# Attention mixer of an encoder trunk: where the two halves of a unit's output are added, and when the output is split

## The chip, the cores and the metric

The kernel runs on one core of a Trainium2 chip. The metric is device microseconds of one execution, as the median of several runs; profiled executions are recorded by the hardware profiler, one at a time.

## What is computed

Two layers of an encoder trunk run on two sequences (512 and 256 tokens, width 1024) with shared weights. Each layer is `x += ½FFN; x += Mixer; x += ½FFN`, each behind an RMSNorm. Layer 0 mixes with a gated linear recurrence, layer 1 with windowed attention; the change lies in the latter:

```python
def window_gqa_mixer(x, w_qkv, w_o, sinks):        # 16 query heads, 4 key heads, d = 64
    q, k, v = split(x @ w_qkv); q, k = rope_partial(q), rope_partial(k)
    # blocks of 128 queries against the block before, their own and the one after
    s = einsum('bnqhgd,bnkhd->bnhgqk', qb, kband) * d**-0.5
    s = where(|kpos - qpos| <= 128, s, -inf)
    m = maximum(max(s), sink); p = exp(s - m)
    o = einsum('bnhgqk,bnkhd->bnqhgd', p / (sum(p) + exp(sink - m)), vband)
    return o.reshape(B, T, 1024) @ w_o
```

All arithmetic is float32 by demand of accuracy. TensorE works on float32r, a shortened form, so every operand is split into a high part `hi` (a cast on ScalarE) and a rest `lo = x - hi` (a subtraction on VectorE), and a product takes two or three matmuls.

## The kernel before

The attention stage (`swa`) starts with the projections of keys and values. Then one hand-made pipeline (`pipeline`) runs 24 units, in each of which one group of four query heads that share a key head meets one block of 128 queries: for each of 4 groups `g`, four blocks of the long sequence and two of the short one. A unit's parts are set on steps, unit `i` starting at step `4 i`:

- `query`, `turn`: split and transpose the queries (`qT`, a buffer of tag `tA`).
- `scores` (L1380, L1381): score matmuls into PSUM, and from there by VectorE (L1383) into a score buffer of tag `big`, with mask and maximum.
- `exps` (L1396) on ScalarE, `sink`, `denominator`: the normalisation runs on GpSimd (L1412), four instructions a unit.
- `probs`, steps 7 to 9: the probabilities are transposed on TensorE (L1418) and split (`split`, L319 and L320) into two `tA` buffers for each block of keys.
- `values`: two matmuls per block of keys (L1430, L1431) accumulate in one PSUM bank, `po`. Its partitions 0 to 63 hold the result with the high part of the values, 64 to 127 that with the low part.
- `finish`, at step `4 i + 8` plus the number of key blocks (2 or 3): ScalarE copies the lower half to partitions 0 to 63 of a `tA` buffer `low` (L1436), and VectorE adds the two halves in two instructions (L1441), even heads to partitions 0 to 63 and odd heads to 64 to 127 of the group's output tile `of`, a `big` buffer.

Between these parts stand the `extra` pieces with steps of their own: the query projection in pieces of six matmuls (the second half of it from step 18 on, every second step, to step 66), a reload of x from DRAM, the output splits and, from step 66 on, 24 pieces of the output projection `out_proj` for its first half, which reads groups 0 and 1. `split_out` casts a group's `of` into high and low parts of two new `big` tiles (L1254 on ScalarE, L1255 on VectorE, four of each for one group). The groups are split at steps 60, 65 and 84, and group 3 behind the pipeline, ahead of the second half of `out_proj`.

The list of events, sorted by step, gives the program order. The framework takes that order as priority, and lays out the queue of each engine by it, by what its own model of durations says is ready, and by which buffers are free: the `big` tag has 21 (h, the normalised input of the projections, takes 8 until the last query block is done), `tA` has 8, PSUM 8 banks. Each engine then works its queue in order. DMAs started on SP or ScalarE are plain; `into` (L147) starts one on GpSimd that adds to its destination. SP's queue also carries all weight loads (L160), and ScalarE and VectorE split the loaded weights (L175, L176).

Of the kernel before, what the change touches and what calls it, by code (L numbers as in the profile page):

```python
# [9 lines left out]
F32 = mybir.dt.float32  # L10
F32R = mybir.dt.float32r
# [5 lines left out]
P = 128  # L17
# [5 lines left out]
T = TA + TB  # L23
# [6 lines left out]
HD = 64  # L30
# [3 lines left out]
SEQS = ((0, TA), (TA, TB))  # L34
# [18 lines left out]
class Trunk:  # L53
# [1129 lines left out]
    def swa(self, next_row):  # L1183
        nc = self.nc
        self.load_bands()
        self.later(self.spill_x)
        kT = [self.big([P, 2, T], F32R) for _ in range(KV)]
        vv = [self.big([P, 3, KV, P], F32R) for _ in range(2)]

        def put_kv(s, b, ps):  # L1190
            off, n = SEQS[s]
            gb = off // P + b
            st = self.big([P, KV, 2, P], F32R)
            kh, kl = st[:, :, 0, :], st[:, :, 1, :]
            k = self.tmp(256)
            self.rotate(ps[:, :256], KV, b, k)
            self.split(k.rearrange("p (h d) -> p h d", d=HD), kh[:, :, :HD], kl[:, :, :HD])
            nc.scalar.copy(kh[:, :, HD:], kh[:, :, :HD].bitcast(F32))
            nc.scalar.copy(kl[:, :, HD:], kl[:, :, :HD].bitcast(F32))
            src = ps[:, 256:].rearrange("p (g d) -> p g d", d=HD)  # L1200
            v = vv[gb // 3][:, gb % 3]
            nc.scalar.copy(v[:, :, :HD], src)
            nc.vector.tensor_sub(v[:, :, HD:], src, v[:, :, :HD].bitcast(F32))

            def rest():
                for g in range(KV):
                    pt = self.ps(256)
                    for i in range(2):
                        self.transpose_r(pt[:, i * P : (i + 1) * P], st[:, g, i, :])
                    nc.scalar.copy(kT[g][:, :, gb * P : (gb + 1) * P], pt.rearrange("p (a b) -> p a b", a=2))  # L1210

            return rest

        self.drain(self.proj_tok("kv", put_kv))
        qtok = {}

        def put_q(half):
            def f(s, b, ps):
                gb = SEQS[s][0] // P + b
                if half and gb % 3 == 0:  # L1220
                    hold.append(self.big([P, 3, 512]))
                t = hold[gb // 3][:, gb % 3] if half else self.xt()[:, :512]
                self.rotate(ps, 512 // HD, b, t)
                for gg in range(2):
                    qtok[(s, b, half * 2 + gg)] = t[:, gg * 256 : (gg + 1) * 256]

            hold = []
            return f

        tiles = [None] * NC  # L1230
        of = {}

        def units(gs):
            def alloc(g):
                if g not in of:
                    of[g] = self.big([P, 2, T])
                return of[g]

            for g in gs:
                for s, (off, n) in enumerate(SEQS):  # L1240
                    for b in range(n // P):
                        q = lambda s=s, b=b, g=g: qtok[(s, b, g)]
                        yield Unit(self, s, b, g, q, kT, vv, lambda g=g: alloc(g))

        def split_out(gs):
            for g in gs:
                for i in range(2):
                    for s, (off, n) in enumerate(SEQS):
                        if s == 0:
                            tiles[2 * g + i] = self.big([P, 2, T], F32R)  # L1250
                        t = tiles[2 * g + i]
                        hi, lo = t[:, 0, off : off + n], t[:, 1, off : off + n]
                        src = of[g][:, i, off : off + n]
                        nc.scalar.copy(hi, src)  # L1254
                        nc.vector.tensor_sub(lo, src, hi.bitcast(F32))  # L1255

        q = itertools.chain(self.proj_tok("q0", put_q(0)), self.proj_tok("q1", put_q(1)))
        wo = self.out_proj("sw_o", 0, tiles, None)
        for _ in range(8):
            next(q)  # L1260
        piece = lambda g: lambda: next(g, None)
        extra = [(i * 5 / 4 - 4, piece(q)) for i in range(16)]
        extra += [(18 + 2 * i, piece(q)) for i in range(25)]
        extra.append((46, self.reload_x))
        extra.append((60, lambda: split_out((0,))))
        extra.append((65, lambda: split_out((1,))))
        extra += [(66 + i * 3 / 2, piece(wo)) for i in range(24)]
        extra.append((84, lambda: split_out((2,))))
        self.pipeline(list(units(range(KV))), extra)
        split_out((3,))  # L1270
        self.drain(wo)
        self.drain(self.out_proj("sw_o", 1, tiles, next_row))

# [44 lines left out]
    def pipeline(self, units, extra):  # L1318
        events = []

        def at(step, rank, *calls):
            events.append((step, rank, len(events), calls))

        for i, u in enumerate(units):
            t = 4 * i
            at(t - (3 if i else 5), 5, u.query)
            at(t - 2, 3.5, u.turn)
            for h in range(GQ):
                at(t + h // 2, 0, lambda u=u, h=h: u.scores(h))
            at(t + 2, 2, u.sink)  # L1330
            for h in range(GQ):
                at(t + 1 + h // 2, 2, lambda u=u, h=h: u.exps(h))
            at(t + 2, 2, u.denominator)
            for j in range(u.nkb):
                at(t + 7 + j, 1, lambda u=u, j=j: u.probs(j))
                at(t + 9 + j, 4, lambda u=u, j=j: u.values(j))
            at(t + 8 + u.nkb, 4, u.finish)
        for step, call in extra:
            at(step, 3, call)
        for _, _, _, calls in sorted(events, key=lambda e: e[:3]):  # L1340
            for c in calls:
                c()


class Unit:
# [87 lines left out]
    def finish(self):  # L1433
        k, nc = self.k, self.k.nc
        low = k.tmp(512)
        nc.scalar.copy(low[:HD, :], self.po[HD:, :])  # L1436
        of = self.of()
        lo = self.off + self.b * P
        for par in range(2):
            r = lambda t: t.rearrange("p (c a q) -> p c a q", a=2, q=P)[:, :, par, :]  # L1440
            nc.vector.tensor_add(of[par * HD : (par + 1) * HD, :, lo : lo + P], r(self.po[:HD, :]), r(low[:HD, :]))  # L1441
# [114 lines left out]
```

## Time and profile before

| | |
|---|---|
| time, median of 3 runs | 2774.59 us (2774.25 to 2774.86) |
| the profiled execution | 2774.57 us, of it 2772.5 us span |
| granted TensorE clock | 0.999 |
| PE busy | 2747.2 us, 99% of the span |
| DVE / ACT / POOL busy | 2220.5 / 1389.7 / 410.5 us |
| attention units, first to last score matmul | 2063.8 to 2228.6 us |
| L1441, the additions of `finish` | 48 of 414 ns |

PE is TensorE's matmuls, PEld its weight loads, DVE VectorE, ACT ScalarE, POOL GpSimd, SP the SyncE that starts most DMAs. In the stretches of time, each engine's busy us are followed by the number of its instructions. In the rows of groups the busy total and the mean of one come first, behind the second bar the engine's idle time just before them and what ended it. In the timeline, the first figure is the start and the second the duration, both in us, and in square brackets stands how long the engine had been idle.

### The profile page before, as it was taken

What the parts mean: (1) busy time and instruction counts of PE and PEld (TensorE: products, weight loads), DVE (VectorE), ACT (ScalarE), POOL (GpSimd) and SP (SyncE); (2) the same over time, 40 slices, a digit from 0 to 9 for tenths busy, and PEclk for the clock granted to TensorE, in tenths of its full rate; (3) what the DMA queues carried; (4) which work ended last, traced back from release to release, by engine and by line L of the source; (5) the groups of instructions that cost most, each with busy time, mean ns of one, the idle gap of its engine ahead of it and who ended that gap; (6) DMA issues with size and microseconds to landing.
All of it is one profiled execution on the core that took longest, in us unless ns stands there. A gap on an engine that the chain in (4) does not pass through costs nothing.

```text
span 2772.5 us, 40790 instructions
## 1 busy us (share of the span) xinstructions
PE 2747.2 (99%) x15117; PEld 2554.7 (92%) x15117; DVE 2220.5 (80%) x3808; ACT 1389.7 (50%) x2589; POOL 410.5 (15%) x449
## 2 busy tenths in 40 slices
PE   8999999999999999999999999999999999999998
PEld 8999999989999889999999999999888789999998
DVE  8788788767887788788878888887848878788877
ACT  7344444734455674444445544444558865444443
POOL 2111121200000101221111121111102211211111
PEclk9999999999999999999999999999999999999999
DMA  6554554851123743555444365544412122655443
GB/s 172 130 126 114 128 138 122 232 155 39 39 62 71 206 116 80 137 137 133 115 115 124 75 147 133 128 116 115 133 66 77 47 65 73 145 133 129 120 112 107
DMA packets 339943, 319.71 MB, mean 115 GB/s; under 512 B 12872, under 2 KB 259104, under 8 KB 339744
## 3 DMA queue, kind: packets, MB, share of 16 engines
q1 hardware_dynamic: 296992, 221.81, 27.2%
q0 software_dynamic: 38448, 81.81, 16.2%
q10 hardware_dynamic: 4304, 13.49, 1.3%
q8 instruction: 119, 1.95, 0.3%
q14 instruction: 80, 0.66, 0.1%
HBM read 225.82 MB, written 15.73 MB: 87 GB/s over the span
## 4 chain that ended last, share of the span: by engine, by line
PE 95%; DVE 2%; ACT 1%; DMA 0%; issue 0%; DVEq 0%; ACTq 0%; SPq 0%
PE ps L513 42%; PE ps L577 21%; PE ps L315 6%; PE ps L314 6%; PE ps L316 6%; PE ps L760 5%; PE ps L823 3%; PE ps L928 1%; PE ps L1418 1%; PE ps L904 1%; PE ps L385 1%; PE ps L1430 0%; PE ps L1380 0%; PE ps L1381 0%; PE ps L1431 0%; PE ps L1181 0%
## 5 line engine op out<-in xcount | busy, mean ns | idle before, releaser
L513 PE MATMUL ps<-big,w 128*128 128x384 f32 x6720 | 1169.3, 334 | 0.0
L513 PEld LDWEIGHTS ps<-big,w 128*128 128x128 f32 x6720 | 1165.9, 188 | 1.7 <-ACT tA L530 0.2
L208 ACT CAST w<-wr 128x512 fp32r<-128x512 f32 x600 | 415.7, 707 | 687.2 <-PE ps L513 279.8
L577 PE MATMUL ps<-w,big 128*128 128x512 f32 x2520 | 575.3, 389 | 0.0
L577 PEld LDWEIGHTS ps<-w,big 128*128 128x128 f32 x2520 | 472.7, 188 | 97.5
L209 DVE TENSOR_TENSOR w<-wr,w 128x512 fp32r<-128x512 f32 (+1 forms) x520 | 437.8, 846 | 147.5 <-ACT w L208 131.5
L599 DVE SCALAR_TENSOR_TENSOR x<-ps,x 128x512 f32<-128x512 f32 x468 | 302.0, 684 | 10.0 <-PE ps L316 9.9
L147 POOL DMA_DIRECT2D s<-wr x126 | 110.5, 884 | 1243.1 <-DMA s<-in_ffn_w_dram 432.8
L314 PE MATMUL ps<-big,w 128*128 128x384 f32 x640 | 219.6, 345 | 1.2 <-ACT w L175 0.9
L315 PE MATMUL ps<-big,w 128*128 128x384 f32 x640 | 215.7, 337 | 0.8 <-DVE big L320 0.8
L316 PE MATMUL ps<-big,w 128*128 128x384 f32 x640 | 214.4, 335 | 0.0
L319 ACT CAST big<-tA 128x384 fp32r<-128x384 f32 x296 | 148.0, 513 | 113.4 <-DVE tA L552 36.2
L760 PE MATMUL ps<-w,big 128*128 128x512 f32 x756 | 177.2, 392 | 0.1
L320 DVE TENSOR_TENSOR big<-tA,big 128x384 fp32r<-128x384 f32 x296 | 169.2, 582 | 6.6 <-ACT big L319 4.6
L147 POOL DMA_DIRECT2D wr<-wr x109 | 95.8, 879 | 524.1 <-DMA wr<-in_ffn_w_dram 191.2
L760 PEld LDWEIGHTS ps<-w,big 128*128 128x128 f32 x756 | 140.5, 188 | 29.2 <-DVE w L320 0.6
L209 POOL TENSOR_TENSOR w<-wr,w 128x512 fp32r<-128x512 f32 x80 | 138.5, 1732 | 195.2 <-ACT w L208 192.2
L215 DVE TENSOR_TENSOR wr<-wr,wr 128x512 f32<-128x512 f32 (+1 forms) x120 | 121.1, 1009 | 24.9 <-issue 21.1
L314 PE MATMUL ps<-w,big 128*128 128x512 f32 x336 | 134.6, 401 | 0.3 <-DVE big L1441 0.2
L316 PE MATMUL ps<-w,big 128*128 128x512 f32 x336 | 132.2, 393 | 0.6 <-DVE big L400 0.5
L315 PE MATMUL ps<-w,big 128*128 128x512 f32 x336 | 131.7, 392 | 0.0
L315 PEld LDWEIGHTS ps<-big,w 128*128 128x128 f32 x640 | 120.5, 188 | 2.1 <-DVE big L320 2.0
(215 smaller groups left out, 3465.8 us busy)
## 6 DMA issues: line engine op xcount, KB each, us to landing
wr<-in_ffn_w_dram SPq DMA_DIRECT2D x264, 512.0 KB, 4.0
s<-wr POOLq DMA_DIRECT2D x126, 256.0 KB, 4.9
s<-in_ffn_w_dram SPq DMA_DIRECT2D x120, 256.0 KB, 3.3
wr<-wr POOLq DMA_DIRECT2D x80, 256.0 KB, 3.8
wr<-in_hg_w_in_dram SPq DMA_DIRECT2D x32, 512.0 KB, 3.9
wr<-wr POOLq DMA_DIRECT2D x29, 512.0 KB, 4.6
spill<-x ACTq DMA_DIRECT2D x12, 512.0 KB, 4.0
kept<-big POOLq DMA_DIRECT2D x8, 768.0 KB, 9.7
```

What stands on the lines that cost most here:

```text
L147: self.nc.gpsimd.dma_start(out, src, accum_op=ALU.add)
L208: nc.scalar.copy(h, src)
L209: (eng or nc.vector).tensor_sub(l, src, h.bitcast(F32))
L314: nc.tensor.matmul(out, a[0], b[0], start=first, stop=False)
L315: nc.tensor.matmul(out, a[0], b[1], start=False, stop=False)
L316: nc.tensor.matmul(out, a[1], b[0], start=False, stop=last)
L319: self.nc.scalar.copy(hi, src)
L320: self.nc.vector.tensor_sub(lo, src, hi.bitcast(F32))
L513: self.nc.tensor.matmul(ps, a[x], b[y], start=first and k == 0 and i == 0, stop=k == 3 and i == 2, skip_group_check=True,)
L577: nc.tensor.matmul(ps, a[x], w[y], start=name == chain and kp == 0 and q == 0, stop=kp == 1 and q == 2, skip_group_check=True,)
L599: self.nc.vector.scalar_tensor_tensor(x, ps, c, x, ALU.mult, ALU.add)
L760: nc.tensor.matmul(ps, x[:, sl], y, start=fresh and k == 0 and q == 0, stop=k == 3 and q == 2, skip_group_check=True,)
```

## The change

For the first 21 units, `finish` copies all 128 partitions of `po` to `low` with one ScalarE instruction. Then, for even and odd heads, a plain DMA on SP writes the upper half of `low` to its place in `of`, and an accumulating DMA on GpSimd adds the lower half to it; each moves 64 partitions of 256 elements. The last three units keep the copy and the two VectorE additions.

`split_out` now does one tile and one sequence at a time. The twelve pieces of groups 0 to 2 stand at steps 50, 52, 54, 56; 58, 60, 62, 64; and 83, 85, 87, 89. Group 3's four pieces stay behind the pipeline.

```diff
-        def split_out(gs):
-            for g in gs:
-                for i in range(2):
-                    for s, (off, n) in enumerate(SEQS):
-                        if s == 0:
-                            tiles[2 * g + i] = self.big([P, 2, T], F32R)
-                        t = tiles[2 * g + i]
-                        hi, lo = t[:, 0, off : off + n], t[:, 1, off : off + n]
-                        src = of[g][:, i, off : off + n]
-                        nc.scalar.copy(hi, src)
-                        nc.vector.tensor_sub(lo, src, hi.bitcast(F32))
+        def split_out(g, i, s):
+            off, n = SEQS[s]
+            if s == 0:
+                tiles[2 * g + i] = self.big([P, 2, T], F32R)
+            hi, lo = (tiles[2 * g + i][:, half, off : off + n] for half in range(2))
+            self.split(of[g][:, i, off : off + n], hi, lo)
...
-        extra.append((60, lambda: split_out((0,))))
-        extra.append((65, lambda: split_out((1,))))
+        for n in range(12):
+            extra.append(((50, 58, 83)[n // 4] + 2 * (n % 4), lambda n=n: split_out(n // 4, n // 2 % 2, n % 2)))
         extra += [(66 + i * 3 / 2, piece(wo)) for i in range(24)]
-        extra.append((84, lambda: split_out((2,))))
         self.pipeline(list(units(range(KV))), extra)
-        split_out((3,))
+        for n in range(4):
+            split_out(3, n // 2, n % 2)
...
         for i, u in enumerate(units):
             t = 4 * i
+            u.moved = i < 21
...
     def finish(self):
         k, nc = self.k, self.k.nc
         low = k.tmp(512)
-        nc.scalar.copy(low[:HD, :], self.po[HD:, :])
         of = self.of()
         lo = self.off + self.b * P
+        if self.moved:
+            nc.scalar.copy(low, self.po)
+            for par in range(2):
+                r = lambda t: t.rearrange("p (c a q) -> p c a q", a=2, q=P)[:, :, par, :]
+                dst = of[par * HD : (par + 1) * HD, :, lo : lo + P]
+                nc.sync.dma_start(dst, r(low[:HD, :]))
+                k.into(dst, r(low[HD:, :]))
+            return
+        nc.scalar.copy(low[:HD, :], self.po[HD:, :])
         for par in range(2):
             r = lambda t: t.rearrange("p (c a q) -> p c a q", a=2, q=P)[:, :, par, :]
             nc.vector.tensor_add(of[par * HD : (par + 1) * HD, :, lo : lo + P], r(self.po[:HD, :]), r(low[:HD, :]))
```

## The prediction

> **What bounds the kernel now.** I read the page's head and chain first, to see which engine has to be relieved for anything to count.
>
> ```profile
> span 2772.5 us, 40790 instructions
> PE 95%; DVE 2%; ACT 1%; DMA 0%; issue 0%; DVEq 0%; ACTq 0%; SPq 0%
> ```
>
> The chain is TensorE's from end to end: 95% of the span. The change takes no matmul away, so all it can give back is time in which TensorE stands still inside the attention stage, and all it can cost is new time of that kind. So next comes the stage itself, cut into stretches of 20 us.
>
> ```profile
> core 0: us, PE busy (x) PEld busy (x) DVE busy (x) ACT busy (x) POOL busy (x), PEclk, DMA share, GB/s
> 2080.00:2100.00 20.00, 19.04 (x112) 15.85 (x110) 17.31 (x50) 16.59 (x42) 5.59 (x9) 1.00 0.33 106
> 2100.00:2120.00 20.00, 19.37 (x116) 16.50 (x114) 14.92 (x53) 16.41 (x47) 6.09 (x14) 1.00 0.24 80
> 2140.00:2160.00 20.00, 19.89 (x117) 17.08 (x116) 16.55 (x59) 16.40 (x48) 6.59 (x14) 1.00 0.01 2
> 2160.00:2180.00 20.00, 17.08 (x94) 13.22 (x92) 18.65 (x55) 18.87 (x49) 4.10 (x8) 1.00 0.31 105
> 2180.00:2200.00 20.00, 19.37 (x109) 15.94 (x110) 17.44 (x55) 14.68 (x43) 5.52 (x12) 1.00 0.00 1
> 2200.00:2220.00 20.00, 20.00 (x115) 17.05 (x114) 17.46 (x49) 16.29 (x43) 5.58 (x8) 1.00 0.23 67
> ```
>
> The other stretches of the stage have PE at 20.00. PE misses 0.96 + 0.63 + 0.11 + 2.92 + 0.63 = 5.25 us, over half of it in 2160 to 2180, where DVE and ACT are both above 18.6 of 20. The waits and the timeline say what happens there.
>
> ```profile
> PE ps L1431 <- DVE tA L320: 2.2, 2, 1.9
> PE ps L1380 <- ACT tA L1371: 0.7, 2, 0.5
> 2170.04 0.39 PE L316 MATMUL ps<-w,big 128*128 128x512 f32 x1
> 2172.32 0.50 PE L1431 MATMUL ps<-tA,big 128*128 128x512 f32 x1 [1.89 <-DVE tA L320]
> 2167.76 1.22 DVE L176 TENSOR_TENSOR w<-wr,w 128x1024 fp32r<-128x1024 f32 x1
> 2168.89 1.96 DVE L1255 TENSOR_TENSOR big<-big,big 128x512 fp32r<-128x512 f32 x4
> 2171.58 0.69 DVE L320 TENSOR_TENSOR tA<-ps,tA 128x512 fp32r<-128x512 f32 x1
> 2179.95 1.95 DVE L1255 TENSOR_TENSOR big<-big,big 128x512 fp32r<-128x512 f32 x4
> ```
>
> The value matmul L1431 waits 1.89 us for the low half of a probability tile (L320). DVE made that late because it had a weight split (L176, 1.22 us) and the four output-split subtractions of group 0 in one lump (L1255, 1.96 us) in front of it. The second lump, group 1's, stands at 2179.95.
>
> Busy time hides a little more: matmuls of this shape start 0.23 us apart in the next fence, so after 2170.04 the next was due at 2170.27 and 2.05 us were lost, 0.16 more than the idle shown. The waits of PE in the stage are nine, so the ceiling of any gain is about 5.25 + 9 x 0.16 = 6.7 us, 0.24% of the run.
>
> ```profile
> 2148.18 0.39 PE L315 MATMUL ps<-w,big 128*128 128x512 f32 x1
> 2148.41 0.40 PE L316 MATMUL ps<-w,big 128*128 128x512 f32 x1
> ```
>
> The Trainium skill, "Perfetto Trace Analysis", section "Identifying the Most-Contended Engine", says that matmul busy time is a bad measure and that weight-load busy time is the better one. By that rule, with the full stretch's PEld of 17.05 as 100%, the four short stretches up to 2200 would lose about 1.4, 0.6, 4.5 and 1.3 us, 7.8 in all, and the ceiling would be 1.1 us higher; no run here shows which is nearer.
>
> The profiled execution took 2774.57 us, 2.07 more than its span; it lies at the median of the three runs (2774.59), so sums made on the trace are put on 2774.6. A difference of 0.2%, 5.5 us, is about what a measurement of this kernel can tell from no change.
>
> **The change part by part.** First the finish of a unit, 21 times.
>
> ```profile
> L319 ACT CAST tA<-ps 128x512 fp32r<-128x512 f32 x56 | 32.7, 585 | 8.7 <-PE ps L1418 8.1
> L1436 ACT COPY tA<-ps 64x512 f32<-64x512 f32 x24 | 14.0, 583 | 3.3 <-PE ps L1431 2.8
> L1441 DVE TENSOR_TENSOR big<-ps,tA 64x256 f32<-64x256 f32 x48 | 19.9, 414 | 4.7 <-ACT tA L1436 4.3
> ```
>
> The ACT copy grows from 64 to 128 partitions. A 128x512 eviction takes 585 ns where the 64x512 one takes 583, so this costs nothing. DVE loses 2 x 414 ns per unit, 42 x 0.414 = 17.4 us over some 140 us; none of it is TensorE time except where DVE is late. The po bank in PSUM comes free after the copy and no longer after the two additions.
>
> In their place stand 42 plain transfers on SP and 42 accumulating ones on GpSimd, 64 KB each. The nearest rows:
>
> ```profile
> big<-in_rope_dram ACTq DMA_DIRECT2D x1, 64.0 KB, 1.9
> wr<-in_sw_w_o_dram SPq DMA_DIRECT2D x8, 512.0 KB, 3.7
> L147 POOL DMA_DIRECT2D s<-wr x126: 855/872/1202, 25.9 to 2712.6; - x126
> DMA to landing us min/median/max: 3.2/4.6/10.7
> 2163.66 11.67 SPq L160 DMA_DIRECT2D wr<-in_sw_w_o_dram  x4
> 2151.79 1.84 POOL L1412 TENSOR_SCALAR big<-big,stat 128x256 f32<-128x256 f32 x4 [3.78 <-DVE stat L1409]
> 2156.48 2.27 POOL L1412 TENSOR_SCALAR big<-big,stat 128x384 f32<-128x384 f32 x4 [2.85 <-PE ps L1418]
> ```
>
> A plain transfer lands in 1.9 us (64 KB) to 3.7 us (512 KB); I take 2, by the row of the same size. An accumulating one occupies GpSimd for 0.87 us and lands 3.2 to 10.7 us later; I take 4, between the smallest and the median, since those rows carry four times the bytes. From the copy's start to the landed sum: 0.58 + 2 + 2 x 0.87 + 4 = 8.3 us, against 0.58 + 0.83 = 1.4 now.
>
> Who is behind these waits? On SP, a plain transfer waits for the copy, and the weight loads stand behind it; there are four of them in 11.67 us, so they have room. On GpSimd, an accumulating transfer waits for the plain one, and behind it stand the next unit's normalisations (L1412). GpSimd is idle 2.85 to 3.78 us between their groups in these rows and needs 1.74 of it. The next copy starts beside a group (2156.37 and 2156.48 below), so the plain transfer lands about when that group ends: hidden, bounds 0 and 2 us per unit, of which I take 0 for most and 0.4 us over the whole stage.
>
> ```profile
> 2156.37 0.58 ACT L1436 COPY tA<-ps 64x512 f32<-64x512 f32 x1
> 2164.18 0.58 ACT L1436 COPY tA<-ps 64x512 f32<-64x512 f32 x1
> ```
>
> Who reads the sum late? The steps are 1.77 us long: score matmuls run from 2063.8 to 2228.6, from step 0 to step 93.
>
> ```profile
> L1380 PE MATMUL ps<-big,tA x96: 274/288/441, 2063.8 to 2228.6; 128*128 128x256 f32 x64, 128*128 128x384 f32 x32
> ```
>
> Unit 11 finishes at step 54 and the first split that reads it is now at 60: 10.6 us for 8.3. Unit 17 finishes at 78 and is read at 85, unit 20 at 91 and is read after 102. All covered; with a landing of 10.7 instead of 4 us the first would not be. The tA buffer of the copy is held 7 us longer, one more of 8 in use for most of a unit; ACT's L319 row above shows no wait for a buffer now, so I cost it at nothing.
>
> Second, the splits. Group 0's moves from one lump at step 60 to four pieces at 50 to 56, group 1's from 65 to 58 to 64, group 2's from 84 to 83 to 89. Work is the same, but 1.96 us of DVE leave the stretch 2160 to 2180, and with two or three finishes there (0.83 each) DVE falls from 18.65 to about 14.5 of 20. L320 at 2171.58 would come 1.96 earlier and the 1.89 us wait is gone. ACT loses its lump too:
>
> ```profile
> 2166.70 1.76 ACT L1254 CAST big<-big 128x512 fp32r<-128x512 f32 x4
> ```
>
> Gains: of the 2.92 us in 2160 to 2180 I take 2.4 (the big wait and half of the rest), of 0.63 behind the second lump 0.4, of the 1.59 in 2080 to 2120 only 0.5, since part of the waits there are for ACT, which keeps its work; and 0.16 for about six waits gone, 1.0. Sum 4.3 us.
>
> Third, a cost that the diff does not show: buffers. The `big` tag has 21. At step 48 the loop holds 8 of h, 4 of keys, 2 of values, the band, 2 of queries and 2 of outputs: 19, which leaves two score buffers. Units hold one from their first score to their last transposed probability. That is tight already:
>
> ```profile
> 2156.70 0.33 PE L1381 MATMUL ps<-big,tA 128*128 128x384 f32 x1
> 2157.22 0.60 PE L1418 MATMUL ps<-ident_r,big 128*128 128x128 f32 x4
> 2158.47 0.61 DVE L1383 CUSTOM_DVE_ANT_0 big<-ps,big,nsinks 128x384 f32<-128x384 f32 x1
> ```
>
> Unit 14's scores are out of TensorE at 2157.0, and DVE starts on them only at 2158.47, after unit 12's last transposes. The change asks for tiles of group 0 at steps 50 and 54, before the first pair of h comes free with the last query block at step 58. Something must wait: the splits (costs nothing) or the scores of units 13 and 14. TensorE has query pieces to run meanwhile, nine of six matmuls, 9 x 6 x 0.23 = 12.4 us, and running them early frees h early. Bounds 0 and 8 us (the rival below); I take 0.3 because the cover is longer than one unit's step of 4 x 1.77 = 7.1 us.
>
> Sum: 4.3 - 0.4 - 0.3 = 3.6 us, 2771.0.
>
> **The rivals.** *Partial cure*, my forecast: 2771.0, anywhere from 2767.5 to 2776.
>
> *Full cure.* Every stall of the stage goes: 2774.6 - 6.7 = 2767.9. For it: DVE is the last releaser in most of the waits. Against it: the waits on ACT (L1380 for L1371, 0.7 us) keep their cause.
>
> *The score buffers become the bound*, between 2147 and 2166. If the two tiles take the freed buffers ahead of units 13 and 14, each starts a unit's step late, 2 x 7.1 = 14.2 us; half of the query pieces cover 6.2. Net +8.0, and of the gain 1.2 us remain: 2781.4. It decides where query pieces are not run ahead of their steps, or where the four score banks that wait in PSUM keep other matmuls from starting. For it: the 1.4 us late start of unit 14 above, already with two buffers. Against it: pieces of 12.4 us cover.
>
> *GpSimd waits.* Plain transfers queue behind the weight loads on SP between 2163 and 2175; they land 2 to 4 us late, GpSimd stands, and the normalisation of three units is late with only a small reserve: unit 11's group ends at 2148.01 and its transposes start at 2149.47.
>
> ```profile
> 2146.17 1.84 POOL L1412 TENSOR_SCALAR big<-big,stat 128x256 f32<-128x256 f32 x4 [5.53 <-DVE big L1441]
> 2149.47 0.60 PE L1418 MATMUL ps<-ident_r,big 128*128 128x128 f32 x4
> ```
>
> 3 units x 2 us = 6 us against the gain of 3.6: 2777.0. The Trainium skill speaks for it: "DMA: Bandwidth & Descriptors", "Rules for kernel authors", says that two transfers to disjoint partition halves serialize, and that under 64 KB one mostly pays overhead, here four transfers of 64 KB for two additions. With its fixed 2 us plus bytes at 436 GB/s, an estimate from that page, the chain would be 0.58 + 2.15 + 0.87 + 2.15 + 0.87 = 6.6 us, shorter than by the rows, so the sum stays. The 64 KB row of 1.9 us agrees.
>
> **How the numbers follow.** Chances: partial cure 0.52, full cure 0.22, score buffers 0.14, GpSimd 0.12. Faster by over 0.2% (below 2769.1): the full cure and 0.04 of the partial one, 0.26. Slower by over 0.2% (above 2780.1): the score buffers and 0.03 of the GpSimd case, 0.17. Within: 0.57. The likeliest case's own range is 2767.5 to 2776; for eight in ten the range takes in the full cure below (2766.0, with the ceiling 2 us too low) and most of the GpSimd case above: 2779.0.
>
> **What would show it.** Right: L1441 with 6 executions; no L1255 lump of 1.9 us; PE in 2160 to 2180 near 19.5; 42 more GpSimd transfers of about 0.87 us, and none among PE's releasers. The score buffers: L1383 late behind L1418 around units 13 to 15 and PE idle there for its operands. GpSimd: L1412 among the releasers of L1418 with the reason a transfer. Wrong altogether: a new wait at ACT for a landing in L1254's place, since everything behind it on ACT would be late.

## The result and the profile after

The changed kernel takes 2768.75 us, the median of 15 runs (2767.49 to 2769.45), beside 2774.67 us before (15 runs, 2774.08 to 2775.81): 5.92 us less. The ratio is 0.9978, with a 95% interval of 0.9970 to 0.9986. The profiled span falls from 2772.5 to 2767.2 us, by 5.3.

First the stretches of the stage that were short before, and 2220 to 2240: time, then busy us of each engine with its number of instructions.

```profile
core 0: us, PE busy (x) PEld busy (x) DVE busy (x) ACT busy (x) POOL busy (x), PEclk, DMA share, GB/s
2080.00:2100.00 20.00, 19.57 (x115) 16.69 (x114) 16.10 (x48) 17.27 (x44) 8.00 (x12) 1.00 0.48 135
2100.00:2120.00 20.00, 20.00 (x121) 17.34 (x120) 13.93 (x52) 16.29 (x50) 14.87 (x24) 1.00 0.58 121
2140.00:2160.00 20.00, 20.00 (x119) 17.37 (x118) 16.82 (x61) 18.82 (x56) 14.40 (x21) 1.00 0.35 50
2160.00:2180.00 20.00, 18.68 (x114) 16.03 (x114) 18.25 (x52) 18.81 (x49) 11.03 (x16) 1.00 0.56 134
2180.00:2200.00 20.00, 20.00 (x115) 17.22 (x114) 13.84 (x45) 13.34 (x40) 12.73 (x20) 1.00 0.32 48
2220.00:2240.00 20.00, 19.58 (x99) 15.74 (x98) 15.26 (x32) 11.43 (x25) 5.14 (x9) 1.00 0.28 59
```

Before, the last of these was whole:

```profile
2220.00:2240.00 20.00, 20.00 (x116) 17.12 (x115) 16.59 (x47) 13.46 (x35) 5.52 (x12) 1.00 0.05 14
```

TensorE misses 0.43 + 1.32 + 0.42 = 2.17 us now, where it missed 5.25. Three of the five short stretches are whole (2100, 2140, 2180), 2080 to 2100 and 2160 to 2180 have lost about half of their holes, and there is a new small one at 2220. DVE is relieved in most stretches, but hardly in 2160 to 2180 (18.25 instead of 18.65), and not in 2140 to 2160 (16.82 instead of 16.55): the pieces and other work have moved up into the place that the lumps left. GpSimd's busy time has more than doubled in the four of these stretches between 2100 and 2200. A stretch does not hold quite the same work as before, since the changed kernel gets ahead by up to 6 us: its last score matmul starts at 2222.4 instead of 2228.6.

The waits of TensorE in the stage, all of them (us in total, times, longest one):

```profile
PE ps L1376 <- ACT tA L1367: 1.3, 2, 1.1
PE ps L1414 <- ACT tA L319: 0.4, 1, 0.4
PE ps L1427 <- DVE tA L320: 0.2, 1, 0.2
PE ps L1426 <- ACT tA L319: 0.2, 1, 0.2
```

Nine waits became five. The 1.9 us behind L320 is gone; the longest is now for ScalarE, which copies the next unit's queries (L1367). Lines from `finish` on have moved: L1376 and L1377 are the score matmuls, L1414 the transposes, L1426 and L1427 the values, L1408 the normalisation.

```profile
L147 POOL DMA_DIRECT2D big<-tA x42: 955/998/1384, 2085.6 to 2224.1; - x42
DMA to landing us min/median/max: 2.5/3.0/4.8
L1439 SPq DMA_DIRECT2D big<-tA x42: 590/599/708, 2082.8 to 2221.5; - x42
DMA to landing us min/median/max: 2.0/2.2/4.7
L1445 DVE TENSOR_TENSOR big<-ps,tA x6: 409/418/418, 2226.0 to 2238.7; 64x256 f32<-64x256 f32 x6
```

Each landing row belongs to the row above it: the plain transfers land in 2.2 us, the accumulating ones take GpSimd 1.0 us each and land 3.0 us later. Six VectorE additions are left.

### The profile page after: what moved, and what is told of

It is laid out like the page before. It is cut to its first block, busy times and chain, and to the rows that moved or that the text cites. A ratio compares the mean times of both kernels' runs of the same rounds, so it can differ in the third digit from the quotient of the medians.

```text
span 2767.2 us, 40933 instructions
## 1 busy us (share of the span) xinstructions
PE 2745.0 (99%) x15117; PEld 2554.8 (92%) x15117; DVE 2206.5 (80%) x3766; ACT 1386.0 (50%) x2589; POOL 453.0 (16%) x491
## 3 DMA queue, kind: packets, MB, share of 16 engines
q0 software_dynamic: 44496, 84.56, 17.4%
## 4 chain that ended last, share of the span: by engine, by line
PE 96%; DVE 2%; ACT 1%; DMA 1%; issue 0%; DVEq 0%; POOL 0%; SPq 0%; ACTq 0%; POOLq 0%
PE ps L513 42%; PE ps L577 21%; PE ps L315 6%; PE ps L316 6%; PE ps L314 6%; PE ps L760 5%; PE ps L823 3%; PE ps L928 1%; PE ps L1414 1%; PE ps L904 1%; PE ps L385 1%; PE ps L1426 0%; PE ps L1376 0%; PE ps L1427 0%; PE ps L1377 0%; PE ps L1181 0%
## 5 line engine op out<-in xcount | busy, mean ns | idle before, releaser
L320 DVE TENSOR_TENSOR big<-tA,big 128x384 fp32r<-128x384 f32 x296 | 168.0, 578 | 6.7 <-ACT big L319 4.7
```

The lines of the kernel that those rows point to most:

```text
L320: self.nc.vector.tensor_sub(lo, src, hi.bitcast(F32))
```

## The experiments

Each was timed in 11 runs beside the kernel before on the same chip, whose median lay between 2774.62 and 2774.84 us in all of them. Line numbers differ by the lines that a run adds: L1427, L1428, L1431 and L1432 are all the value matmul that reads L320's low half, L1376, L1377 and L1380 the score matmul that waits for the queries' copy, and L1367, L1368 and L1371 that copy.

**The transfers alone.** The kernel before with the new `finish`; the splits stay in lumps.

```diff
+            u.moved = i < 21
...
         extra.append((60, lambda: split_out((0,))))
         extra.append((65, lambda: split_out((1,))))
```

> The kernel before with the new finish alone; the splits stay in lumps at steps 60, 65 and 84. Theory (VectorE's backlog in front of the probability splits is what TensorE waits for, and each part of the change shortens it by about its own share): the lump of 1.96 us stays in front of L320, so the 1.89 us wait shrinks only by the additions no longer in front of it, 0.83 to 1.7 us; about 2.5 us gained in all, 2772. Rival 1 (the transfers do it all): 2769. Rival 2 (the pieces do it all, the transfers only add waits on GpSimd): 2774.7 or later.

2771.09 us (2769.61 to 2772.74), ratio 0.9987 (0.9978 to 0.9995): 3.7 us gained. One row of its stretches:

```profile
2160.00:2180.00 20.00, 17.87 (x102) 14.07 (x102) 18.60 (x51) 18.93 (x49) 9.97 (x14) 1.00 0.51 131
```

And one of TensorE's waits:

```profile
PE ps L1432 <- DVE tA L320: 1.0, 2, 0.8
```

The value matmuls' wait for L320 is halved, not gone, while 2100 to 2160 and 2180 to 2200 are already whole. That is the theory's picture, with a larger gain.

**The pieces alone.** The changed kernel with all units added on VectorE.

```diff
-            u.moved = i < 21
+            u.moved = False
```

> The changed kernel with no unit moved: all 24 units add on VectorE, the splits stand in pieces. Theory: the lump is gone from the queue ahead of L320, the additions stay; about 3 us gained, 2771.5. Rival 1 (the transfers do it all): 2774.7. Rival 2 (the pieces do it all): 2769.

2772.38 us (2771.62 to 2773.29), ratio 0.9992 (0.9983 to 1.0001): 2.4 us, at the edge of what the interval can tell. Two of its stretches:

```profile
2080.00:2100.00 20.00, 19.05 (x111) 15.87 (x111) 17.28 (x49) 16.61 (x42) 6.01 (x10) 1.00 0.35 109
2160.00:2180.00 20.00, 18.24 (x105) 14.53 (x104) 19.44 (x58) 17.97 (x47) 4.93 (x8) 1.00 0.32 105
```

And the wait in question:

```profile
PE ps L1427 <- DVE tA L320: 0.2, 1, 0.2
```

Here the wait for L320 has gone from 2.2 to 0.2 us, and the stretches around 2100, where no split stands, are as short as before. The two parts cure mostly different places, and their gains add up: 3.7 + 2.4 = 6.1 beside 5.9 for both. Neither rival holds: no run of either part alone was as fast as any of the changed kernel, or as slow as any of the kernel before. But by its interval the gain of the pieces alone is not clear of zero.

**The lump moved, not cut.**

```diff
-        extra.append((60, lambda: split_out((0,))))
+        extra.append((50, lambda: split_out((0,))))
```

> The kernel before with group 0's split, still one lump, at step 50 in place of 60. If the lump in front of L320 is what made the 1.89 us wait, that wait goes, and 2 us with it: 2772.6. If the wait is due to the stretch being full (weight splits, scores, projections), it stays in another place: 2774.7.

2773.15 us (2772.30 to 2774.30), ratio 0.9995 (0.9986 to 1.0004): 1.6 us, which the interval can't tell from none. TensorE's waits are plainer than the time:

```profile
PE ps L1380 <- ACT tA L1371: 1.1, 2, 0.8
PE ps L1431 <- DVE tA L320: 0.3, 1, 0.3
```

The crowded stretch beside them:

```profile
2160.00:2180.00 20.00, 18.51 (x100) 14.34 (x99) 19.38 (x57) 19.24 (x50) 5.24 (x9) 1.00 0.32 106
```

L320's wait falls from 2.2 to 0.3 us by this move alone, so the lump in front of it was its cause. A part comes back as a longer wait for ScalarE, 0.7 to 1.1 us.

**All 24 units.**

```diff
-            u.moved = i < 21
+            u.moved = True
```

> The changed kernel with all 24 units joined by transfers. The last unit's sum is read at once by group 3's splits, and the second half of the output projection stands behind those. Theory: the chain of copy, plain and accumulating transfer (0.58 + about 2.2 + 2 x 1.0 + 3 us, as the rows of the changed kernel have them) stands open at the end of the pipeline, less the first-half projection pieces that are left: 2 to 6 us slower than the changed kernel, 2771 to 2775. Rival (24 are as good as 21): 2768 to 2769.

2769.25 us (2768.72 to 2770.40), ratio 0.9981 (0.9972 to 0.9989). The theory was wrong here: 24 can't be told from 21. By busy time the open end costs TensorE about half a microsecond, 0.90 us missing in 2220 to 2240 instead of 0.42, by the row of that stretch:

```profile
2220.00:2240.00 20.00, 19.10 (x97) 15.46 (x96) 12.90 (x26) 9.81 (x22) 8.64 (x13) 1.00 0.43 80
```

**One buffer less.**

```diff
-SLOTS = 21
+SLOTS = 20
```

> The changed kernel with 20 big buffers in place of 21. In its trace the tiles of tag big that are alive number 21 at most, from 2149 to 2157, since the keys of groups 0 and 1 are done by then. Theory (the score buffers are not the bound: one buffer less makes one tile wait a few us, and query pieces cover it): within 1 us of the changed kernel, 2768 to 2770. Rival (the early pieces live off the last free buffer): a unit's scores start late and at least half a unit's step is lost, 2772 or more.

2774.76 us (2774.07 to 2775.28), ratio 0.9999 (0.9991 to 1.0008): the whole gain is gone, as the rival said. But the constant holds for the entire kernel. The rows of the score matmuls, of the changed kernel and then of this one, say where:

```profile
L1376 PE MATMUL ps<-big,tA x96: 274/286/424, 2064.2 to 2222.4; 128*128 128x256 f32 x64, 128*128 128x384 f32 x32
```

```profile
L1376 PE MATMUL ps<-big,tA x96: 277/288/423, 2066.4 to 2226.1; 128*128 128x256 f32 x64, 128*128 128x384 f32 x32
```

The first score matmul is 2.2 us late before the stage has begun, the last 3.7; of the 4.9 us by which the span is longer, 1.5 fall between them and 1.2 behind. So this run mixes stages, and the next two hold a buffer in the stage alone.

**One or two buffers held through the stage.** Eight columns of each are set at the stage's start and touched at its end; the second run has `range(2)`.

```diff
+        held = [self.big([P, 2, T]) for _ in range(1)]
+        for t in held:
+            nc.gpsimd.memset(t[:, 0, :8], 0.0)
...
         self.pipeline(list(units(range(KV))), extra)
+        for t in held:
+            nc.vector.tensor_add(t[:, 0, :8], t[:, 0, :8], of[3][:, 0, T - 8 : T])
```

> The changed kernel with one of the 21 big buffers held idle through the attention stage alone (eight columns set at its start and touched at its end). In the run with 20 buffers the first score matmul came 2.2 us late already, and the last 3.7 us late, so some 1.5 us of its loss arose in the stage. Theory (in the stage one buffer less costs little, the rest was lost in other stages): 2769 to 2770.5. Rival (the score buffers are the bound): 2772 or more.

> As the run before, with two buffers held: 19 are left where the changed kernel has 21 alive from 2149 to 2157. Theory: now a score buffer is missing for a good part of a unit's step, 3 to 8 us slower than the changed kernel, 2772 to 2777, with the loss between 2140 and 2180. Rival (query pieces run early cover this too): 2770 or less.

2770.77 us (2770.13 to 2771.60) with one, 2773.88 us (2772.77 to 2775.32) with two: 2.0 and 5.1 us above the changed kernel; the ratios to the kernel before are 0.9986 (0.9977 to 0.9995) and 0.9997 (0.9988 to 1.0006). The first lies a little beyond the theory's 2770.5 and short of the rival's 2772, the second inside the theory's. With two held, the stretches and the longest wait:

```profile
2140.00:2160.00 20.00, 19.63 (x110) 15.83 (x109) 12.52 (x41) 14.58 (x43) 12.79 (x18) 1.00 0.36 50
2160.00:2180.00 20.00, 17.00 (x94) 13.24 (x93) 19.59 (x59) 19.34 (x52) 9.83 (x14) 1.00 0.45 127
```

```profile
PE ps L1432 <- DVE tA L320: 1.6, 2, 1.4
```

I read this as the look of a lack of buffers: VectorE and ScalarE run dry (12.52 and 14.58 of 20) while a unit waits for room, and are overfull 20 us later, when TensorE pays. The changed kernel has none to spare. The few instructions that set and touch the held buffers are in these times too.

**Twice the issues for GpSimd.** The plain transfers are issued there too.

```diff
-                nc.sync.dma_start(dst, r(low[:HD, :]))
+                nc.gpsimd.dma_start(dst, r(low[:HD, :]))
```

> The changed kernel with the plain transfers issued by GpSimd too, 42 more issues of about 1.0 us there: from 2100 to 2180 GpSimd goes from about 13 to about 18 us busy in 20. Theory (GpSimd has room between the normalisations and these have 0.5 to 7 us in hand before TensorE reads them): the reserve is used up at some units, 1 to 4 us slower than the changed kernel, 2770 to 2773. Rival (GpSimd's waits already cost the changed kernel a part of its gain): twice the issues cost much more, 2775 or later. Rival 2 (its load is free throughout): 2769.

2778.35 us (2777.09 to 2780.48), ratio 1.0013 (1.0004 to 1.0022): 9.6 us above the changed kernel, and slower than before. The crowded stretch, then waits of TensorE, then the group of the 256-wide normalisations (count, busy us, mean ns, idle before them):

```profile
2160.00:2180.00 20.00, 15.53 (x81) 12.16 (x80) 15.09 (x39) 14.54 (x36) 15.01 (x22) 0.94 0.50 113
```

```profile
PE ps L1426 <- ACT tA L319: 2.9, 3, 1.8
PE ps L1427 <- DVE tA L320: 2.1, 4, 0.9
PE ps L1414 <- POOL big L1408: 1.0, 4, 0.4
```

```profile
L1408 POOL TENSOR_SCALAR big<-big,stat 128x256 f32<-128x256 f32 x64 | 39.8, 977 | 107.8 <-ACT tA L1367 101.5 <-PE ps L1414 3.2 <-DVE stat L1405 3.1
```

VectorE and ScalarE are no longer full (about 15 of 20), and TensorE misses 4.5 us. TensorE now waits for GpSimd itself, though longer for the splits on ScalarE and VectorE; that those are late by a chain that begins at GpSimd is likely, but not shown apart. The 9.6 us are not the price of the issues alone: GpSimd also stands longer for landings (30.2 us instead of 21.0), and the granted clock was 0.94 in this stretch and 0.98 in the next, where the changed kernel has 1.00. The reserve that hides 42 issues doesn't hide 84. In the changed kernel itself no instruction of TensorE waits for GpSimd, and VectorE waits 2.2 us for it (1.2 before). So GpSimd's own cost there is small; that it is nil was not shown.

**The copy on VectorE, always and for every second block.**

```diff
-            nc.scalar.copy(low, self.po)
+            nc.vector.tensor_copy(low, self.po)
```

The second run does this for odd blocks alone.

> The changed kernel with the 128x512 copy of a moved unit made by VectorE and not by ScalarE. In the changed kernel TensorE's longest wait is for ScalarE (the queries' copy, 1.1 us at 2170), and ScalarE is at 18.8 of 20 from 2140 to 2180 with VectorE at 14 to 18. Theory (ScalarE is late next): ScalarE loses 21 x 0.59 us, VectorE gets 21 x about 0.69 back; 1 us faster than the changed kernel, 2767.5 to 2768.5. Rival (VectorE is still as near to the bound, so that whatever is put back on it costs): 2770 to 2771.

> As the run before, but with VectorE making the copy for every second block alone (blocks 1 and 3 of the long sequence, 1 of the short one). Theory: the load is shared most evenly, 2767.5 to 2768.5, no later than with all copies on VectorE. Rival (it is no matter of load but of a few places): equal to the changed kernel, 2768.8.

2770.12 us (2769.35 to 2770.54) and 2770.56 us (2770.08 to 2771.10); ratios 0.9982 (0.9973 to 0.9991) and 0.9985 (0.9976 to 0.9994). Against the changed kernel's 0.9978 the intervals overlap, but neither is faster, and the theory that ScalarE's load is what is late falls. The first came where its rival had it, the second where neither of its forecasts had it. With all copies on VectorE, a stretch and TensorE's longest wait:

```profile
2140.00:2160.00 20.00, 19.36 (x111) 16.50 (x110) 18.14 (x58) 16.01 (x47) 12.93 (x19) 1.00 0.32 46
```

```profile
PE ps L1376 <- ACT tA L1367: 2.6, 4, 1.2
```

With the copies on VectorE, ScalarE has 16.01 where it had 18.82, and TensorE's wait for it has doubled from 1.3 to 2.6 us. A busy share doesn't say what is in front of the late instruction.

**Group 0's pieces earlier; the splits of the output projection's weights in halves.**

```diff
-            extra.append(((50, 58, 83)[n // 4] + 2 * (n % 4), lambda n=n: split_out(n // 4, n // 2 % 2, n % 2)))
+            extra.append(((46, 58, 83)[n // 4] + 2 * (n % 4), lambda n=n: split_out(n // 4, n // 2 % 2, n % 2)))
```

> The changed kernel with group 0's four pieces at steps 46 to 52 in place of 50 to 56, four steps (some 7 us) further from the crowded stretch 2160 to 2180. Theory (ScalarE and VectorE are late in that stretch alone, and it no longer holds these pieces): no more than 0.5 us either way, 2768.3 to 2769.3. Rival (the pieces still push work into that stretch, or take a buffer from the scores too early): a change of over 1 us, down or up.

2768.56 us (2768.05 to 2769.61), ratio 0.9979 (0.9971 to 0.9988): the same as the changed kernel, as the theory had it.

```diff
-            self.nc.scalar.copy(hi, raw)
-            self.nc.vector.tensor_sub(lo, raw, hi.bitcast(F32))
+            for part in [slice(i, i + 1) for i in range(2)] if key[0] == "sw_o" else [slice(None)]:
+                self.nc.scalar.copy(hi[:, part], raw[:, part])
+                self.nc.vector.tensor_sub(lo[:, part], raw[:, part], hi[:, part].bitcast(F32))
```

> The changed kernel with each of the eight splits of the output projection's weights in two halves of 512 columns (cast on ScalarE, subtraction on VectorE). In the changed kernel the queries' copy L1367, for which TensorE waits 1.10 us at 2170.20, stands behind one such cast of 1.03 us. Theory (what is late next is a single large instruction in front of a small urgent one, as with the lump before): 0.5 to 1 us faster than the changed kernel, 2767.8 to 2768.3. Rival (the engines are full there, and two halves cost more than one whole): 2769 or more.

2769.78 us (2768.12 to 2770.60), ratio 0.9981 (0.9972 to 0.9990): no gain. Two of TensorE's waits:

```profile
PE ps L1377 <- ACT tA L1368: 1.1, 2, 0.9
PE ps L1428 <- DVE tA L321: 0.6, 2, 0.3
```

The wait for the queries' copy fell from 1.3 to 1.1 us only, and that for the probability split rose from 0.2 to 0.6. No version beats the changed kernel by anything that these runs can tell.

## Why the prediction was right, point by point

**Direction and place.** It forecast 2771.0 in a range of 2766.0 to 2779.0, and 2768.75 came: inside the range, but just below 2769.1, where the forecast had put a chance of 0.26, and not in the middle, where it had put 0.57. The named wait was the right one: L320 behind the lump, shown by moving the lump alone. Its share was not. The sum took 2.8 of its 3.3 us of idle time from the stretches of the lumps, but the pieces alone gave 2.4 us and the transfers alone 3.7. And the picture of 2160 to 2180 failed: VectorE was to fall to about 14.5 us there and TensorE to come to 19.5, and they came to 18.25 and 18.68. The forecast took group 0's lump out of that stretch and did not put group 1's four pieces in, whose steps 58 to 64 lie there:

```profile
L320 DVE TENSOR_TENSOR big<-big,big 128x512 fp32r<-128x512 f32 (+1 forms) x4 | 2.2, 554 | 0.0
```

**The gain, 4.3 us in the sum.** It was too small; 5.9 us is nearer to the full cure (6.7) than to the 3.6 that the sum left after its costs, though five waits remain. By PE's busy time the terms compare so: 2160 to 2180, 2.4 taken and 1.60 measured; behind the second lump 0.4 and 0.63; 2080 to 2120, 0.5 and 1.16; nothing taken for 2140 to 2160 and 0.11 measured; and 0.42 lost at 2220 that the sum did not have. Together 3.1 us, while the span fell by 5.3. The term that failed most is the last one, 1.0 us for what busy time hides: 2.2 are left for it, though only four waits went and not six. So the time came within the range by the range's width: the sum was 2.3 us short, its terms missed in both directions, and no run shows the costs of 0.4 and 0.3 us apart.

The Trainium skill's rule ("Perfetto Trace Analysis", "Identifying the Most-Contended Engine") sizes the gain better: by an estimate with 17.05 as full, PEld now misses about 0.4 (2080), 1.2 (2160) and 1.5 us (2220), 3.1 where it missed 7.8. That is 4.7 of the 5.3 us, where matmul busy time shows 3.1. Other traces bear it out: over 2060 to 2240, with PEld's change put on the same scale, it gives 5.5 us for the changed kernel's 5.3 of span, 3.5 for 3.3 with the transfers alone, 3.8 for 4.2 with all copies on VectorE and 0.9 for 0.9 with two buffers held. With the pieces alone it falls short, 2.1 for 3.0, and it doesn't fit the runs with 20 buffers or with 84 issues, where other stages or the clock change too. A single stretch is sized less surely, since stretches with PE at 20.00 have between 16.3 and 17.4 us of PEld in these traces.

The additions, 3.7 us by themselves, were under-sized too: in 2080 to 2120 I left two thirds of the loss standing because ScalarE keeps its work, and with the transfers alone 2100 to 2120 was whole. The one wait there was for a cast of probabilities on ScalarE. The same cast before, and with the transfers alone, 1.9 us earlier:

```profile
2107.46 0.58 ACT L319 CAST tA<-ps 128x512 fp32r<-128x512 f32 x1
2105.56 0.58 ACT L319 CAST tA<-ps 128x512 fp32r<-128x512 f32 x1
```

Before, exponentials stood in front of it on ScalarE, and the scores that they read stood behind additions on VectorE. So work that ScalarE keeps came earlier all the same; that this chain is the whole reason was not tested apart.

**What is late next.** The sum left half of the rest in 2160 to 2180 without a name. In the changed kernel's timeline it is this:

```profile
2168.18 0.45 PE L1181 MATMUL ps<-ident_r,s 128*128 128x128 f32 x4
2168.64 1.03 ACT L175 CAST w<-wr 128x1024 fp32r<-128x1024 f32 x1
2169.57 0.57 ACT L1367 CAST tA<-ps 128x512 fp32r<-128x512 f32 x1
2170.20 0.38 PE L1376 MATMUL ps<-big,tA 128*128 128x256 f32 x1 [1.10 <-ACT tA L1367]
```

The queries are transposed at about 2168.6, and ScalarE then casts a weight for 1.03 us before it copies them. Cutting that cast in two and giving ScalarE less to do both failed to help; in both runs a cast of weights still stood in front of the queries' copy. So what would remove this wait stays open.

**The score buffers.** The count of 19 was wrong: the keys of group 0 and of group 1 return their tiles when the group's last scores are done. From the first write to the last read of every `big` tile, at most 20 were alive before and 21 are now, at times from 2149 to 2157. There are only 21, so this count can't show that no tile waited. The row read as a sign of shortage was wrong too. VectorE was not idle for want of a buffer at unit 14, it was busy, as its timeline of before has it:

```profile
2156.99 0.85 DVE L1441 TENSOR_TENSOR big<-ps,tA 64x256 f32<-64x256 f32 x2 [0.70 <-ACT tA L1436]
2157.86 0.69 DVE L320 TENSOR_TENSOR tA<-ps,tA 128x512 fp32r<-128x512 f32 x1
2158.47 0.61 DVE L1383 CUSTOM_DVE_ANT_0 big<-ps,big,nsinks 128x384 f32<-128x384 f32 x1
```

None of TensorE's five waits is for a score buffer, so the small price (0.3 us) fits, but for want of a shortage and not for the cover named. The mechanism is real all the same: two buffers fewer bring 5.1 us of the 8 us that the rival priced.

**GpSimd and the chain of transfers.** Issue 0.87 taken, 1.0 measured; plain landing 2 and 2.2; accumulating landing 4 and 3.0: the chain is 0.58 + 2.2 + 2 x 1.0 + 3.0 = 7.8 us for 8.3. The copy of 128 partitions cost nothing more, as taken: 587 ns, where that of 64 took 583. GpSimd does stand for landings, without a wait of TensorE for it:

```profile
POOL big L147 <- DMA big<-tA: 21.0, 11, 4.7
```

The first half of the rival was there at 42: two plain transfers, issued at 2163.26 and 2171.82 among weight loads on SP, landed 4.1 and 4.4 us later instead of 2.2, and GpSimd stood 2.32 and 4.21 us. The second half, TensorE waiting for a late normalisation, did not come with them. It came with 84 issues (1.0 us), not by way of SP's queue, and with two buffers held (0.7 us).

**The readers of the sum.** "All covered" failed once, at unit 20. The first split of group 3 was put in ScalarE's queue ahead of the pipeline's end and met a transfer that had not landed (timeline):

```profile
2227.68 0.62 ACT L319 CAST big<-big 128x512 fp32r<-128x512 f32 x1 [1.73 <-DMA big<-tA]
```

Its copy had started 7.5 us earlier, at 2220.2. This is the wait at ScalarE that was named as what would be wrong altogether, and right behind it stands the cast for which TensorE waits first in the new hole at 2220:

```profile
2228.33 0.58 ACT L319 CAST tA<-ps 128x512 fp32r<-128x512 f32 x1
2228.96 0.50 PE L1426 MATMUL ps<-tA,big 128*128 128x512 f32 x1 [0.20 <-ACT tA L319]
```

With the transfers alone ScalarE has such a wait too (1.8 us) and the stretch misses 0.53 us; with the pieces alone the stretch is whole. So the transfers bring this loss, most likely by that wait; a run that takes away the wait alone was not made.

## What to carry to other kernels

A saturated engine's short waits are found by asking what stood in front of the late instruction on the other engine's queue, and one lump of operations there can be worth cutting or moving even if its total stays. Ask also what the pieces land on: here group 1's filled the stretch that group 0's lump had left. Taking 17 us of additions off an engine that is only now and then late bought 3.7 us, while the helper engine and the buffer pool had just enough left: test both by taking some away before building further on them. For the ceiling of a gain on TensorE, read weight-load busy time beside matmul busy time, over the whole stage.

## What the runs showed of the hardware

A mean of GpSimd's records can mislead. The mean of a 128x256 normalisation is 497 ns before, 772 ns with 42 issues on the same engine and 977 ns with 84. The groups, before and after:

```profile
L1412 POOL TENSOR_SCALAR big<-big,stat 128x256 f32<-128x256 f32 x64 | 30.6, 497 | 176.4 <-ACT tA L1371 112.7 <-DVE stat L1409 15.2 <-PE ps L1381 13.7
```

```profile
L1408 POOL TENSOR_SCALAR big<-big,stat 128x256 f32<-128x256 f32 x64 | 35.8, 772 | 112.9 <-ACT tA L1367 101.8 <-PE ps L1414 6.0 <-DVE stat L1405 4.9
```

But the changed kernel's timeline of GpSimd shows that little or no time is lost by it:

```profile
2176.84 1.98 POOL L147 DMA_DIRECT2D big<-tA  x2 [4.21 <-DMA big<-tA]
2178.10 2.56 POOL L1408 TENSOR_SCALAR big<-big,stat 128x256 f32<-128x256 f32 x4
```

The group of four begins 0.72 us before the second issue's record ends, at 2178.82, and ends at 2180.66: 1.84 us behind the issue, and 1.84 us is what such a group took with no issue in front of it. So the record of an instruction behind an issue begins while the issue's record still runs, the four records overlap, and their mean rises without more work. Busy time, in which overlaps count once, rises from 49.84 to 93.73 us for GpSimd between 2060 and 2240. That is 43.9 us for 42 issues, 1.05 each, where their own row has a median of 1.0.
